# A two-block transformer kernel: first loads on two queues, one load for x and its weights, new durations in the list scheduler

## The chip, the core and the metric

The kernel runs on 1 core of one Trainium2 chip. A core has five engines with instruction streams of their own: PE (TensorE, matmuls), DVE (VectorE), ACT (ScalarE), POOL (GpSimd) and SP (SyncE, which here only issues loads and stores). The metric is the device time of one execution in microseconds (us), the median of the runs; lower is better.

## The reference

256 rows of 1,024 features pass through two transformer blocks in f32. What the start of the program computes is the first normalisation and the first product:

```
def rmsnorm(x, w):
    xf = x.astype(jnp.float32)
    y = xf * lax.rsqrt(jnp.mean(xf * xf, axis=-1, keepdims=True) + EPS)
    return (y * w.astype(jnp.float32)).astype(x.dtype)

def first_block(x, attn_norm_w, w_in, ...):
        h = rmsnorm(x, attn_norm_w[l])
        proj = h @ w_in[l]
        (q_a, k_a, v_a, q_b, k_b, v_b, g_b, g_c, x_c) = jnp.split(proj, split_points, axis=-1)
        y_sb = from_heads(stick_breaking_attention(to_heads(q_a), to_heads(k_a), to_heads(v_a)))
        qh = rmsnorm(to_heads(q_b), q_norm_w[l])
        kh = rmsnorm(to_heads(k_b), k_norm_w[l])
        y_ch = from_heads(chunked_relpos_attention(qh, kh, to_heads(v_b), rel_bias[l]))
        y_cv = short_conv_mixer(g_b, g_c, x_c, conv_w[l])
        y = group_rmsnorm(jnp.concatenate([y_sb, y_ch, y_cv], axis=-1), out_norm_w[l])
        x = x + y @ w_out[l]
        x = x + swiglu(rmsnorm(x, ffn_norm_w[l]), w_gate[l], w_up[l], w_down[l])
    return x
```

The second block (a gated spatial mixer, a dilated attention, a convolved feed-forward part) follows in the same way. About 124 MB of weights and tables are read once.

## The kernel before, in words

**Tiles.** The 256 rows are two tiles of 128 (t = 0 and 1). Every product is done as three f32r products: the operands are split into a rounded high part and a low part (the remainder), and high by high, low by high and high by low are added up in PSUM. x comes already transposed (`xT`, features on the partitions), in four pieces of 256 KB: `xT00` and `xT01` are the two halves of the features for t = 0, `xT10` and `xT11` those for t = 1 (first digit t, second digit the half). `first_half` loads a piece, multiplies it by the norm's weights (`vec`, a table of all such weights), makes the high part on ACT and the low part on DVE. The row scale of the norm comes from X (x, not transposed) and is put on later, when the sums leave PSUM.

**Weights.** They stand in DRAM in the order of use, cut into units of 512 KB (256 features by 512 columns). `load_stream` (L499) issues them on SP into a ring of 4 buffers (`raw`); `hi_stream` makes the high part on ACT (`whi`), `lo_stream` the low part on DVE (`wlo`), each in a ring of 8. A unit costs each row tile 6 matmuls of 128x512 (4 with `whi`, 2 with `wlo`). Units 0 and 1 (`FINE = 2`) are loaded and split in two halves of 256 KB, a and b below. The table `START` (L33) says ahead of which unit the other first loads are issued. Nine bf16 matmuls on zeros (`warm`, `WARM = 9`) run ahead of everything on PE.

**Order.** The program is written by a list scheduler (`Kit.run`, L385): streams of operations are Python generators, every operation has an engine and an estimated duration, and the one that could start first by these estimates is written next. So the estimates decide the order of every engine's instructions, and on the chip each engine works in that order, waiting on semaphores. `evac` (L341) also uses the estimates: what has to leave PSUM goes to ACT or to DVE, whichever is free first. `get` gives out buffers of a ring in the same way, by the estimated time at which they come free.

**Queue.** All loads and stores are issued on SP. Its stream is in order too: an issue whose buffer isn't free yet holds up all issues behind it.

Of the kernel before, what the change touches and what calls it, by code (L numbers as in the profile page):

```python
# [13 lines left out]
ALU = mybir.AluOpType  # L14
# [18 lines left out]
START = {0: ("xT00",), "half": ("xT00b",), 1: ("xT10",), 3: ("xT01",), 4: ("xT11",), 5: ("X0",), 7: ("X1",),  # L33
         8: ("W", "cst"), 9: ("rel",), 16: ("cw",)}
# [134 lines left out]
class Op:  # L169
    __slots__ = ("eng", "cost", "ins", "outs", "fn", "table")  # L170

    def __init__(self, eng, cost, ins, outs, fn, table=None):
        self.eng, self.cost, self.fn, self.table = eng, cost, fn, table
        self.ins = [x.cell for x in ins if isinstance(x, T)]
        self.outs = [x.cell for x in outs if isinstance(x, T)]
# [13 lines left out]
class Kit:  # L189


    def __init__(self, nc, pool, psum):
        self.nc, self.pool, self.psum = nc, pool, psum
        self.clk = {e: 0.0 for e in ("pe", "act", "dve", "pool", "dma")}
# [60 lines left out]
    def mm(self, *items, also=()):  # L255
        cost, ins, outs = 0.0, list(also), []
        for out, a, b, start, stop in items:
# [4 lines left out]
            elif dt == BF16:  # L262
                cost += 0.42e-3 * max(n, 64)
            elif raw(out).shape[0] == 64:
                cost += 0.133
            else:
                cost += 4 * 0.417e-3 * max(n, 128)
# [9 lines left out]
    def tr(self, ident, *items):  # L277
# [4 lines left out]
        return Op("pe", 0.106 * len(items), [a for _, a in items], [o for o, _ in items], fn)  # L282
# [66 lines left out]
    def dma(self, out, in_, eng="dma", nbytes=None):  # L349
# [20 lines left out]
    def emit(self, op, start):  # L370
# [6 lines left out]
        if op.eng == "dma":  # L377
            end += 2.0
# [35 lines left out]
def build(ctx, tc, a):  # L414
# [48 lines left out]
    qk8 = fixed("qk8", [P, 2])  # L463
    stats = fixed("stats", [P, 256])
# [34 lines left out]
    def load_stream():  # L499
        def first(*names):  # L500
            for n in names:
                if n == "W":
# [5 lines left out]

        for p in range(NU):
# [153 lines left out]
    def run_units(t, seq, pt, tag, fin, src=None):  # L663
# [3 lines left out]
        for i, (name, c, u) in enumerate(seq):  # L667
# [6 lines left out]
            else:  # L674
                if i == 0 and (t, tag) == (0, "n1"):
                    yield from k.until("px0")
                    xs = [(px[0][0][:, j], px[0][1][:, j]) for j in (0, 1)]
# [688 lines left out]
    px = {}  # L1366

    def first_half(t, h, pt, ss):
# [3 lines left out]
        yield from k.until(f"go_xT{t}{h}")  # L1372
        xw = yield from k.get("xw", [P, 4, P])
        cuts = [(0, 2), (2, 4)] if (t, h) == (0, 0) else [(0, 4)]
        parts = [xw.part((slice(None), slice(i, j))) for i, j in cuts]
        if len(cuts) == 2:
            yield k.dma(vec, a["vec"])
        for (i, j), part in zip(cuts, parts):
            if i:
                yield from k.until("go_xT00b")  # L1380
            yield k.dma(part, a["xT"][:, t, 4 * h + i:4 * h + j])
            k.done(f"xT{t}{h}" + ("b" if i else ""))
        for (i, j), part in zip(cuts, parts):
            w = V_ATTN + 4 * h
            hi, lo = pt[h][1][:, i:j], pt[h][2][:, i:j]
            if len(cuts) == 2:
                hi, lo = [T(v.ap, Cell()) for v in (hi, lo)]
                px[i // 2] = (hi, lo)
            yield k.tt(part, part, vec[:, w + i:w + j].bc(2, [P, j - i, P]), ALU.mult)
            yield k.act(hi, part)  # L1390
            yield k.tt(lo, part, hi.f32(), ALU.subtract)
            if len(cuts) == 2:
                k.done(f"px{i // 2}")
        k.free(xw, *parts)
        if len(cuts) == 2:
# [319 lines left out]
```

## Time and profile before

| | |
|---|---|
| median of 3 runs | 707.07 us (706.31 to 707.54) |
| profiled execution, its own time | 707.77 us |
| its span, first to last instruction | 706.0 us |
| PE busy | 688.6 us (98% of the span) |
| DVE busy | 488.1 us (69%) |
| ACT busy | 395.5 us (56%) |
| POOL busy | 59.6 us (8%) |
| read from HBM | 123.94 MB |

The profile is of one execution. Between its span and its own time lie 1.77 us outside the first and the last instruction, and its own time is 0.70 us above the median of the runs. Busy is the share of time in which an engine has an instruction under way; a matmul that runs at half clock counts as busy for twice as long.

### The profile page before, as it was taken

What the parts mean: (1) busy time and instruction counts of PE and PEld (TensorE: products, weight loads), DVE (VectorE), ACT (ScalarE), POOL (GpSimd) and SP (SyncE); (2) the same over time, 40 slices, a digit from 0 to 9 for tenths busy, and PEclk for the clock granted to TensorE, in tenths of its full rate; (3) what the DMA queues carried; (4) which work ended last, traced back from release to release, by engine and by line L of the source; (5) the groups of instructions that cost most, each with busy time, mean ns of one, the idle gap of its engine ahead of it and who ended that gap; (6) DMA issues with size and microseconds to landing.
All of it is one profiled execution on the core that took longest, in us unless ns stands there. A gap on an engine that the chain in (4) does not pass through costs nothing.

```text
span 706.0 us, 9657 instructions
## 1 busy us (share of the span) xinstructions
PE 688.6 (98%) x3535; PEld 573.3 (81%) x3535; DVE 488.1 (69%) x743; ACT 395.5 (56%) x614; POOL 59.6 (8%) x105
## 2 busy tenths in 40 slices
PE   7999999999999999999999999999999999999995
PEld 3878777888888888888887888888888888888884
DVE  5666777687666666686567556457777878777773
ACT  4667674565545544574457647444546756555542
POOL 0461433010000000011000000000011000000001
PEclk8999999999999999999999999999999999999998
DMA  7883435555555555565454355665454555555531
GB/s 217 323 273 120 146 121 186 180 208 176 174 208 185 182 180 182 196 228 167 139 187 154 94 179 174 213 206 179 162 179 167 172 178 189 179 191 197 188 110 60
DMA packets 38392, 126.17 MB, mean 179 GB/s; under 512 B 4668, under 2 KB 6856, under 8 KB 38344
## 3 DMA queue, kind: packets, MB, share of 16 engines
q1 hardware_dynamic: 38344, 125.54, 53.0%
q8 instruction: 28, 0.46, 0.3%
q14 instruction: 20, 0.16, 0.1%
HBM read 123.94 MB, written 1.06 MB: 177 GB/s over the span
## 4 chain that ended last, share of the span: by engine, by line
PE 89%; DMA 4%; DVE 2%; ACT 2%; issue 1%; POOL 1%; SPq 0%; POOLq 0%; ACTq 0%; DVEq 0%
PE acc L273 50%; PE work L273 35%; PE work L280 3%; DMA raw<-in_weights 2%; DVE wlo L301 1%; ACT whi L293 1%; DMA xw<-in_xT 1%; DMA uvB<-uvA 1%; POOL stats L301 1%; ACT xw L293 0%; SPq L355 0%; DVE X L301 0%; DVE xw L301 0%; POOL uvB L301 0%; ACT s L293 0%
## 5 line engine op out<-in xcount | busy, mean ns | idle before, releaser
L301 DVE TENSOR_TENSOR wlo<-raw,whi 128x1024 fp32r<-128x1024 f32 (+1 forms) x230 | 275.8, 1208 | 86.9 <-ACT whi L293 69.0
L293 ACT ACTIVATE whi<-raw 128x1024 fp32r<-128x1024 f32 (+1 forms) x230 | 235.1, 1042 | 102.9 <-PE acc L273 74.8
L273 PE MATMUL acc<-whi,xb 128*128 128x512 f32 (+1 forms) x768 | 201.1, 392 | 4.0 <-ACT whi L293 3.8
L273 PEld LDWEIGHTS acc<-whi,xb 128*128 128x128 f32 x768 | 141.4, 189 | 36.0 <-ACT whi L293 6.9
L273 PE MATMUL work<-xb,whi 128*128 128x512 f32 x576 | 143.4, 391 | 0.0
L273 PEld LDWEIGHTS work<-xb,whi 128*128 128x128 f32 x576 | 105.9, 188 | 20.6
L273 PE MATMUL acc<-wlo,xb 128*128 128x512 f32 (+1 forms) x384 | 116.0, 398 | 3.1 <-DVE wlo L301 3.1
L273 PEld LDWEIGHTS acc<-wlo,xb 128*128 128x128 f32 x384 | 69.3, 190 | 18.3 <-DVE wlo L301 4.9
L273 PEld LDWEIGHTS work<-xb,wlo 128*128 128x128 f32 x576 | 78.5, 190 | 5.6
L273 PE MATMUL work<-xb,wlo 128*128 128x256 f32 x576 | 80.4, 282 | 0.0
L301 POOL TENSOR_SCALAR stats<-stats 128x1 f32<-128x1 f32 (+3 forms) x36 | 15.3, 424 | 592.5 <-ACT xw L293 555.2
L273 PE MATMUL acc<-whi,qkb 128*128 128x512 f32 x224 | 59.7, 390 | 0.0
L273 PEld LDWEIGHTS acc<-whi,qkb 128*128 128x128 f32 x224 | 41.3, 188 | 8.1
L293 ACT ACTIVATE qka<-work 128x256 f32<-128x256 f32 (+1 forms) x56 | 19.5, 380 | 43.3 <-PE work L273 38.7
L273 PE MATMUL acc<-wlo,qkb 128*128 128x512 f32 x112 | 34.6, 393 | 0.0
L301 DVE TENSOR_TENSOR qka<-work,qka 128x256 f32<-128x256 f32 (+1 forms) x56 | 22.1, 419 | 17.3 <-ACT qka L293 17.2
L273 PE MATMUL acc<-whi,y 128*128 128x512 f32 x96 | 25.9, 391 | 0.0
L301 POOL TENSOR_TENSOR stats<-stats,half 128x1 f32<-128x1 f32 (+3 forms) x26 | 25.0, 960 | 2.0
L293 ACT ACTIVATE xb<-xw 128x512 fp32r<-128x512 f32 (+1 forms) x21 | 12.8, 610 | 21.4 <-DVE xw L301 21.3
L293 ACT ACTIVATE xw<-X 128x512 bf16<-128x512 f32 x20 | 12.5, 626 | 20.9 <-DVE X L301 20.9
L273 PEld LDWEIGHTS acc<-wlo,qkb 128*128 128x128 f32 x112 | 20.5, 188 | 3.9
L301 DVE TENSOR_TENSOR qka<-qka,s 128x512 f32<-128x512 f32 x27 | 18.7, 693 | 6.2 <-ACT qka L293 5.6
(204 smaller groups left out, 642.9 us busy)
## 6 DMA issues: line engine op xcount, KB each, us to landing
raw<-in_weights SPq DMA_DIRECT2D x222, 512.0 KB, 4.1
raw<-in_weights SPq DMA_DIRECT2D x8, 256.0 KB, 2.6
X<-in_x SPq DMA_DIRECT2D x4, 256.0 KB, 6.3
s<-relext SPq DMA_DIRECT2D x4, 256.0 KB, 5.4
out<-y SPq DMA_DIRECT2D x4, 256.0 KB, 2.1
xw<-in_xT SPq DMA_DIRECT2D x3, 256.0 KB, 6.8
cB<-in_final_norm_g SPq DMA_DIRECT2D x1, 512.0 KB, 5.4
uvB<-uvA SPq DMA_DIRECT2D x4, 112.0 KB, 3.8
```

The source lines that it names most:

```text
L273: self.nc.tensor.matmul(raw(out), raw(a), raw(b), start=start, stop=stop, skip_group_check=True)
L280: self.nc.tensor.transpose(raw(out), raw(a), raw(ident))
L293: self.nc.scalar.activation(raw(out), raw(in_), func, scale=raw(scale), **kw)
L301: getattr(e, meth)(*[raw(x) for x in a], **{k: raw(v) for k, v in kw.items()})
```

## The change

1. The first piece of x and the first eight norm weights become one array, `xT00`, of 520 floats per partition, loaded by one transfer; the load of `vec` moves from the first place to the one ahead of unit 5. The load of unit 0's first half is issued by ACT, all others by SP.
2. ACT's activation table is loaded by a small activation on `half` ahead of the wait for x. The four blocks of 128 columns of the first piece are scaled and rounded by ACT, one activation each (`activation` with a scale per partition), and DVE makes each low part from the unscaled x in one operation (`scalar_tensor_tensor`). The matmuls of t = 0 wait for blocks, not for pieces. The other pieces use a copy of the weights made on POOL (`wn1`).
3. `xT10` and `xT11` land in the buffers `yb0` and `yb1`, no longer in the ring `xw`.
4. The scheduler's estimates change: a load costs its issue (0.45), then a wire that all loads share (1.4 and the bytes at 330 GB/s); the clocks start at 0.7; small f32 matmuls, transposes, POOL and the first nine matmuls get other durations.

```diff
-START = {0: ("xT00",), "half": ("xT00b",), 1: ("xT10",), 3: ("xT01",), 4: ("xT11",), 5: ("X0",), 7: ("X1",),
-         8: ("W", "cst"), 9: ("rel",), 16: ("cw",)}
+START = {1: ("xT10",), 3: ("xT01",), 4: ("xT11",), 5: ("vec",), 6: ("X0",), 7: ("X1",), 8: ("W", "cst"), 9: ("rel",), 16: ("cw",)}
+
+D_ISSUE, D_LAT, D_BYTE, T0 = 0.45, 1.4, 1 / 330e3, 0.7
...
-            return 0.12 + 2.2e-3 * n
+            return 0.28 + 2.2e-3 * n
...
-            self.nc.sync.dma_start(raw(out), raw(in_))
-
-        return Op(eng, max(nbytes / 360e3, 0.1), [in_], [out], fn)
+            (self.nc.scalar if eng == "act" else self.nc.sync).dma_start(raw(out), raw(in_))
+
+        return Op(eng, D_ISSUE, [in_], [out], fn, nbytes=nbytes)
...
-        if op.eng == "dma":
-            end += 2.0
+        if op.nbytes:
+            self.wire = end = max(self.wire, end + D_LAT) + op.nbytes * D_BYTE
...
+        yield from k.until("x00")
         for p in range(NU):
             yield from first(*START.get(p, ()))
             r = yield from k.get("raw", [P, 2, width[p]])
             rawt[p] = (r, halves(r, p))
             for i, d in enumerate(rawt[p][1]):
-                yield k.dma(d, src_of[p] if p >= FINE else src_of[p][:, i:i + 1])
-                if p == 0 and i == 0:
-                    yield from first(*START["half"])
+                yield k.dma(d, src_of[p] if p >= FINE else src_of[p][:, i:i + 1], "dma" if p or i else "act")
...
-        cuts = [(0, 2), (2, 4)] if (t, h) == (0, 0) else [(0, 4)]
...
+        if (t, h) == (0, 0):
+
+            xs = yield from k.get("s", [P, 4 * P + 8])
+            yield k.dma(xs, a["xT00"])
+            k.done("x00")
+            w8 = xs[:, 4 * P:4 * P + 8]
+
+            yield from k.until("half")
+            yield k.act(qk8[:, 0:1], half[:, 0:1])
+            px = PX[t]
+            for i in range(4):
+                px[i] = [T(pt[h][n].ap[:, i], Cell()) for n in (1, 2)]
+                src, sc = xs[:, P * i:P * i + P], w8[:, i:i + 1]
+                yield k.act(px[i][0], src, AF.Copy, sc)
+                yield k.stt(px[i][1], src, sc, px[i][0].f32(), ALU.mult, ALU.subtract)
+                k.done(f"px{t}{i}")
+            yield k.copy(wn1, w8, "pool")
...
+            xw = yield from k.get(f"yb{h}" if t else "xw", [P, 4, P])
+            yield k.dma(xw, a["xT"][:, t, 4 * h:4 * h + 4])
+            k.done(f"xT{t}{h}")
+            yield from k.until("w8")
+            yield k.tt(xw, xw, wn1[:, 4 * h:4 * h + 4].bc(2, [P, 4, P]), ALU.mult)
```

What the change does to the order of the instructions stands in the built programs. First SP's stream, from its start, before. Names are tiles (`raw_0` is the first buffer of the ring `raw`, the numbers behind it count uses), `xw`, `s` and `yb0` are the buffers that x lands in, sizes are partitions by elements:

```order
L355 DMA vec_74<-in_vec 128x134
L355 DMA xw_0_20_99<-in_xT 128x256
L355 DMA raw_0_24_104<-in_weights 128x512
L355 DMA xw_0_20_99<-in_xT 128x256
L355 DMA raw_0_24_104<-in_weights 128x512
L355 DMA xw_1_29_117<-in_xT 128x512
L355 DMA raw_1_30_124<-in_weights 128x512 x2
L355 DMA raw_2_32_132<-in_weights 128x1024
L355 DMA xw_0_34_142<-in_xT 128x512
L355 DMA raw_0_35_150<-in_weights 128x1024
L355 DMA xw_1_37_156<-in_xT 128x512
L355 DMA raw_1_41_171<-in_weights 128x1024
```

SP's stream from its start, of the change:

```order
L357 DMA s_1_20_100<-in_xT00 128x520
L357 DMA raw_0_24_104<-in_weights 128x512
L357 DMA yb0_0_26_108<-in_xT 128x512
L357 DMA raw_1_27_113<-in_weights 128x512 x2
L357 DMA raw_2_31_121<-in_weights 128x1024
L357 DMA xw_0_32_124<-in_xT 128x512
L357 DMA raw_3_33_128<-in_weights 128x1024
L357 DMA yb1_0_34_133<-in_xT 128x512
L357 DMA raw_0_37_154<-in_weights 128x1024
L357 DMA vec_74<-in_vec 128x134
L357 DMA raw_1_40_174<-in_weights 128x1024
```

Three issues have gone from the front (`vec`, a half of x, a half of unit 0, which is ACT's now). Unit 3 took the buffer of unit 0 (`raw_0`) and takes the unused fourth one now (`raw_3`); no piece of x lands any more in a buffer that another piece had, where `xT01` and `xT11` did.

ACT's stream from its start, before:

```order
L293 ACT_TABLE_LOAD
L293 ACTIVATE xb0_67<-xw_0_20_99 128x256
L293 ACTIVATE whi_0_25_105<-raw_0_24_104 128x512
L293 ACTIVATE xb0_67<-xw_0_20_99 128x256
L293 ACTIVATE whi_0_25_105<-raw_0_24_104 128x512
L293 ACTIVATE xb0_67<-xw_1_29_117 128x512
L293 ACTIVATE whi_1_33_140<-raw_1_30_124 128x512 x2
```

ACT's stream from its start, of the change:

```order
L357 DMA raw_0_24_104<-in_weights 128x512
L295 ACT_TABLE_LOAD
L295 ACTIVATE qk8_78<-half_75 128x1
L295 ACTIVATE xb0_67<-s_1_20_100 128x128 x4
L295 ACTIVATE whi_0_25_105<-raw_0_24_104 128x512 x2
L295 ACTIVATE whi_1_36_147<-raw_1_27_113 128x512
L295 ACTIVATE xb0_67<-yb0_0_26_108 128x512
L295 ACTIVATE whi_1_36_147<-raw_1_27_113 128x512
```

All four blocks of x stand ahead of the first `whi` now, where one half of them did; the table load was ACT's first instruction already.

Third, DVE in the attention part of the first block, t = 1 (`pt` is the transposed softmax, copied out of PSUM; `y1` its output), before:

```order
L301 TENSOR_TENSOR wlo_6_156_787<-raw_2_125_593,whi_6_155_785 128x1024
L301 TENSOR_TENSOR uvA0_0_8_87<-uvA0_0_8_87,uvB0_0_9_88 128x256
L301 ISA s_0_154_772,stats_79<-work_0_151_763,cA_0_73_332 128x256
L301 ISA stats_79 128x1
L301 RECIPROCAL stats_79<-stats_79 128x2
L301 TENSOR_TENSOR wlo_7_161_817<-raw_0_139_670,whi_7_159_814 128x1024
```

The same place in DVE's stream, of the change:

```order
L303 TENSOR_TENSOR wlo_6_148_749<-raw_2_122_579,whi_6_147_742 128x1024
L303 TENSOR_TENSOR uvA0_0_8_88<-uvA0_0_8_88,uvB0_0_9_89 128x256
L303 COPY pt_2_149_756<-work_0_141_695 128x512
L303 RECIPROCAL stats_80<-stats_80 128x2
L303 COPY pt_3_154_779<-work_2_142_696 128x512
L303 RECIPROCAL stats_80<-stats_80 128x2
L303 TENSOR_TENSOR wlo_7_153_773<-raw_3_131_635,whi_7_152_771 128x1024
```

Copies of `pt` that ACT made stand on DVE now: in this part of the program DVE has 5 of them where it had 2, and two more products of 256 columns leave PSUM by DVE. PE's matmuls are the same ones. Of the 1,986 rows of its stream, the order differs from the 28th to about the 216th (the first block up to its output product), from the 1,029th to the 1,155th (the second block's attention) and in one row further on; the rest is the same, the end included.

## Rows read from the trace of the kernel before

**Rows 1.** The page: PE's busy time, its share of the span, its instructions.

```profile
PE 688.6 (98%) x3535; PEld 573.3 (81%) x3535; DVE 488.1 (69%) x743; ACT 395.5 (56%) x614; POOL 59.6 (8%) x105
```

**Rows 2.** PE's waits, whole run: us in total, times, the longest.

```profile
PE acc L273 <- ACT whi L293: 3.8, 2, 2.4
PE acc L273 <- DVE wlo L301: 3.1, 3, 1.4
...
PE work L280 <- DVE qkb L301: 1.0, 1, 1.0
```

**Rows 3.** Timeline from the start: start, us, engine, line, operation, tiles [idle before <-releaser].

```profile
0.71 1.28 ACT L293 ACT_TABLE_LOAD   x1 [0.71 <-PEq L1705]
0.72 0.39 SPq L355 DMA_DIRECT2D vec<-in_vec  x1
...
1.17 4.02 PE L273 MATMUL work<-pt 128*128 128x512 bf16 x9 [1.17 <-DVE pt L301]
...
2.58 0.43 SPq L355 DMA_DIRECT2D raw<-in_weights  x1
...
5.31 0.73 PE L273 MATMUL acc<-whi,xb 128*128 128x512 f32 x2
...
7.79 0.63 ACT L293 ACTIVATE whi<-raw 128x512 fp32r<-128x512 f32 x1 [1.70 <-DMA raw<-in_weights]
...
8.47 1.12 PE L273 MATMUL acc<-whi,xb 128*128 128x512 f32 x2 [2.42 <-ACT whi L293]
...
10.69 0.68 DVE L301 TENSOR_TENSOR wlo<-raw,whi 128x512 fp32r<-128x512 f32 x1
...
11.41 0.33 SPq L355 DMA_DIRECT2D raw<-in_weights  x1
...
11.43 0.80 PE L273 MATMUL acc<-wlo,xb 128*128 128x512 f32 x1 [1.42 <-DVE wlo L301]
...
15.53 1.53 PE L273 MATMUL acc<-whi,xb 128*128 128x512 f32 x6
```

**Rows 4.** Longest pieces of the chain after 60 us: start, us, what.

```profile
437.65 44.94 PE acc L273 x198
```

**Rows 5.** Stretches: us, busy us (instructions) of each engine, granted clock, DMA.

```profile
core 0: us, PE busy (x) PEld busy (x) DVE busy (x) ACT busy (x) POOL busy (x), PEclk, DMA share, GB/s
0.00:1.70 1.70, 0.53 (x2) 0.26 (x3) 0.27 (x1) 0.99 (x1) 0.79 (x7) 1.00 0.00 0
1.70:5.20 3.50, 3.49 (x9) 0.90 (x7) 0.85 (x2) 1.17 (x3) 0.00 (x0) 1.00 0.76 213
5.20:8.60 3.40, 0.86 (x3) 0.43 (x4) 1.36 (x3) 1.10 (x3) 0.00 (x0) 1.00 0.88 189
8.60:12.00 3.40, 1.98 (x4) 0.88 (x4) 1.82 (x3) 1.19 (x3) 0.00 (x0) 0.50 0.75 292
12.00:15.50 3.50, 3.50 (x9) 2.80 (x9) 3.50 (x6) 2.17 (x3) 0.00 (x0) 0.51 0.77 239
...
20.00:27.00 7.00, 6.94 (x31) 5.30 (x30) 3.67 (x3) 5.78 (x13) 3.26 (x9) 1.00 1.04 393
...
80.00:120.00 40.00, 36.93 (x202) 30.53 (x201) 29.60 (x53) 24.21 (x44) 12.01 (x19) 1.00 0.46 154
```

**Rows 6.** Groups by shape, ACT and DVE: xcount | busy us, mean ns.

```profile
L293 ACT ACTIVATE whi<-raw 128x512 fp32r<-128x512 f32 x8 | 4.9, 624 | 4.2 <-PE acc L273 2.5 <-DMA raw<-in_weights 1.7
...
L293 ACT ACTIVATE vb<-vb,vec 128x128 f32<-128x128 f32 x8 | 3.0, 396 | 0.8 <-DVE vb L301 0.8
...
L293 ACT ACTIVATE yb<-work 128x128 fp32r<-128x128 f32 x4 | 1.1, 277 | 1.8 <-PE work L273 1.7
...
L301 DVE SCALAR_TENSOR_TENSOR vb<-xw,vec,vb 128x128 f32<-128x128 f32 x16 | 5.6, 350 | 0.4
...
L301 DVE COPY pt<-work 128x512 f32<-128x512 f32 x5 | 3.4, 685 | 0.8 <-PE work L280 0.8
```

**Rows 7.** DMA issues from 3.5 to 6 us: KB each, median us to landing.

```profile
raw<-in_weights SPq DMA_DIRECT2D x2, 256.0 KB, 7.2
```

More of the change, by code (lines that the diff above doesn't have):

```diff
@@ L169, with __init__ @@
 class Op:
[L170 to L173 removed]
+    __slots__ = ("eng", "cost", "ins", "outs", "fn", "table", "nbytes")
+    def __init__(self, eng, cost, ins, outs, fn, table=None, nbytes=0):
+        self.eng, self.cost, self.fn, self.table, self.nbytes = eng, cost, fn, table, nbytes
         self.ins = [x.cell for x in ins if isinstance(x, T)]
@@ L252, in spawn, with mm @@
         self.streams.append([prio, gen, None])
-    def mm(self, *items, also=()):
-        cost, ins, outs = 0.0, list(also), []
+    def mm(self, *items, also=(), more=0.0):
+        cost, ins, outs = more, list(also), []
         for out, a, b, start, stop in items:
@@ L263, in mm @@
                 cost += 0.42e-3 * max(n, 64)
-            elif raw(out).shape[0] == 64:
-                cost += 0.133
+            elif raw(out).shape[0] == 64 or raw(a).shape[0] == 64:
+                cost += 0.108 if n <= 128 else 2 * 0.422e-3 * n
             else:
-                cost += 4 * 0.417e-3 * max(n, 128)
+                cost += 0.224 if n <= 128 else 4 * 0.422e-3 * n
             ins += [a, b]
@@ L501, in first @@
             for n in names:
-                if n == "W":
+                if n == "vec":
+                    yield k.dma(vec, a["vec"])
+                    k.done("vec")
+                elif n == "W":
                     yield k.dma(W, a["cst"][:, C_W + 2:C_W + P + 2])
@@ L674, in run_units @@
             else:
-                if i == 0 and (t, tag) == (0, "n1"):
-                    yield from k.until("px0")
-                    xs = [(px[0][0][:, j], px[0][1][:, j]) for j in (0, 1)]
+                if u < 2 and (t, tag) == (0, "n1"):
+                    yield from k.until(f"px{t}{2 * u}", f"px{t}{2 * u + 1}")
+                    xs = [PX[t][2 * u], PX[t][2 * u + 1]]
                 else:
@@ L1371, in first_half @@
         pt[h] = (x, x.part((slice(None), 0)), x.part((slice(None), 1)))
-        yield from k.until(f"go_xT{t}{h}")
-        xw = yield from k.get("xw", [P, 4, P])
-        cuts = [(0, 2), (2, 4)] if (t, h) == (0, 0) else [(0, 4)]
[L1375 to L1393, printed above, removed]
@@ L1394, in first_half @@
-        k.free(xw, *parts)
-        if len(cuts) == 2:
+        if (t, h) == (0, 0):
[13 more added lines that the diff above has]
+            yield k.copy(wn1, w8, "pool")
+            k.done("w8")
@@ L1396, in first_half @@
             for n in (1, 2):
-                pt[h][n].cell.w = max(px[0][n - 1].cell.w, px[1][n - 1].cell.w)
+                pt[h][n].cell.w = max(px[i][n - 1].cell.w for i in range(4))
                 pt[h][n].cell.eng = "act" if n == 1 else "dve"
+            k.free(xs)
+        else:
+            yield from k.until(f"go_xT{t}{h}")
+            xw = yield from k.get(f"yb{h}" if t else "xw", [P, 4, P])
[3 more added lines that the diff above has]
+            yield k.tt(xw, xw, wn1[:, 4 * h:4 * h + 4].bc(2, [P, 4, P]), ALU.mult)
+            yield k.act(pt[h][1], xw)
+            yield k.tt(pt[h][2], xw, pt[h][1].f32(), ALU.subtract)
+            k.free(xw)
@@ L1559, in setup @@
         yield k.memset(half, -0.5, "pool")
+        k.done("half")
         yield from k.until("x0")
@@ L1629, in warm @@
         for i in range(WARM):
-            yield k.mm((b, z[:, 0:P], z, True, True))
+            yield k.mm((b, z[:, 0:P], z, True, True), more=0.21)
         k.free(b)
@@ L1694 @@
         "xT": v["x"].reshape(2, P, 8, P).transpose(3, 0, 2, 1),
+        "xT00": np.concatenate([v["x"].reshape(2, P, 8, P).transpose(3, 0, 2, 1)[:, 0, 0:4].reshape(P, 4 * P),
+                                vec[:, 0:8]], axis=1),
         "vec": vec,
```

8 lines of the change are left out of this document (5 added, 3 removed).

## The prediction

> **What bounds the kernel now.** I read the page first: PE is busy in 98% of the span [rows 1], so a change can gain where PE waits, where it runs at half clock, or by fewer matmuls. The matmuls are the same. The list of PE's waits [rows 2] shows three kinds: for the rounded weights (`whi`, 3.8 us in 2 waits), for the remainders (`wlo`, 3.1 us in 3) and one of 1.0 us for `qkb`. The timeline [rows 3] puts the longest of the first two kinds into the first 12 us: 2.42 us ahead of 8.47 and 1.42 us ahead of 11.43. That leaves 1.4 + 1.7 + 1.0 = 4.1 us for all that comes later.
>
> The start costs more than these waits. The first real matmul starts at 5.31, and the six that start at 15.53 come after 2+2+1+1+6+2 = 14 of them (the timeline's rows between, of which [rows 3] shows the ends of the waits). Far on in the run, 198 matmuls of the same size take 44.94 us, 0.227 us each [rows 4]. So 15.53 - 5.31 = 10.22 us did 14 x 0.227 = 3.18 us of work: **7.04 us are lost**, 3.84 in the two waits and 3.2 in matmuls that took twice as long. The stretches [rows 5] show why: the granted clock is 1.00 until 8.6 us, 0.50 from 8.6 to 12.0 and 0.51 to 15.5, that is 1.2 GHz in place of 2.4; PE had been busy for 0.86 of 3.40 us before it fell, and for a whole stretch before it came back.
>
> Why is the data late? The second half of unit 0 is issued as the fifth load, at 2.58 us, and ACT waits for it until 7.79 [rows 3]. The DMA engines are busy for 0.76 to 0.88 of the time from 1.7 us on but move 189 to 292 GB/s, where they move 393 at 20 to 27 us [rows 5]; the halves of unit 1 land 7.2 us after their issue [rows 7]. And unit 3, which took unit 0's buffer, is issued at 11.41, when the second `wlo` of unit 0, begun at 10.69, is through [rows 3]; SP had been standing at this row with all later loads behind it.
>
> **The change part by part, against the 7.04 us.**
>
> *First matmul.* The piece of x (266 KB) and the first half of unit 0 (262 KB) go out together at about 0.72 us, from two queues. The engines begin to move data at 1.7 us [rows 5]. 528 KB take 1.34 us at 393 GB/s and 2.48 us at 213: x is there between 3.1 and 4.2, I take 3.7. Then ACT has four blocks of 128 columns, for which the trace has 277 ns without and 396 ns with an operand per partition [rows 6]: 1.1 to 1.6 us, I take 1.3, nearer to the second since these have a scale. Then `whi`, 0.62 [rows 6]: 5.65 us, against 5.31. **+0.3 us** (from -0.1, since the nine matmuls on zeros end at 1.17 + 4.02 = 5.19 [rows 3], to +1.1).
>
> The Trainium skill, "DMA: Bandwidth & Descriptors", section "Issuing engines are not separate DMA queues", says that loads started from several engines run on the same 16 DMA engines and interleave, and that only the time to start them is saved. By that rule the sum is the one above; if the second queue had engines of its own, x would land after its own 266 KB, at 2.4 to 2.9 us, and the first matmul would wait for the matmuls on zeros alone, at 5.2. No run so far has loads on two queues.
>
> *Issues and the table.* The issue on ACT takes some 0.4 us as SP's do, ahead of a table load of 1.28 [rows 3]; both end at about 2.4, before x is there, as the dummy activation does. The table load was over early before, too: this part is worth nothing, and would cost 0.4 us if x landed before 2.4. `vec` (69 KB, 0.2 us at 393 GB/s) goes from the first place on SP to the one ahead of unit 5; its next reader, on POOL, stands behind the row sums of X, which are loaded later still. POOL's copy of the weights runs while `xT10`, its first user's other operand, is on its way; without that cover it would cost its own few tenths. Nothing is taken for these.
>
> *The second half of unit 0* is second in SP's queue. 790 KB are through at 3.7 (393 GB/s) to 5.4 us (213 GB/s). Its `whi` follows the first on ACT, at 6.3. DVE's four remainders of x take 0.35 us each [rows 6], beside ACT's blocks, and end before it. The wait of 2.42 us is gone, and t = 0 has its six matmuls of unit 0 done at about 7.3.
>
> *Unit 1.* Next come `xT10` and the halves of unit 1, up to 1,314 and 1,577 KB. At the rates of the trace (1.7 to 5.2: 745 KB; to 8.6: 643 more; then 292 GB/s [rows 5]) they land at 8.2 and 9.25; at 393 GB/s at 5.1 and 5.7. I take 7.0 and 8.0, between the two, since the slow stretch has less to explain it when issues don't stand still. With 0.62 for `whi`, PE gets its matmuls at 7.6 and 8.6, and unit 2 (2,101 KB, 7.1 to 11.0, then 1.06 us of `whi`) just about as it is through with these and with t = 1 on unit 0. PE's order here is that of before. **2.0 us of waits are left** (0.3 to 3.9), for 3.84. Units 3 and 4 and both other pieces of x have free buffers or nearly so; from there on the loads should keep ahead: a unit lasts 12 x 0.227 = 2.7 us on PE and 524 KB take 2.2 us even at 239 GB/s.
>
> *Clock.* Before, 0.86 us of matmul stood in the 3.4 us ahead of the fall; now it would be some 2. Whether that holds the clock no row says: the 1.98 us in the next stretch, already at half clock, did not bring it back. Lost is nothing, or half of a stretch of 3.4 us, 1.7, or both stretches as before, 3.3. I take half of 1.7: **0.9 us**.
>
> Sum of the start: 0.3 + 2.0 + 0.9 = 3.2 us lost for 7.04: **3.8 us gained.**
>
> *The new estimates* change the order up to the attention of the first block, and in the second block's, where PE has no wait to win. Three more copies of `pt` at 0.685 us [rows 6] and two products of 256 columns move from ACT to DVE: 2.1 us for the copies alone, 3.0 with the others at half a copy and more each, on an engine that is busy for 29.6 of 40 us from 80 to 120 us [rows 5]. PE waits for `wlo` there, but the 4.1 us of later waits could as well shrink under better estimates. I take **0** (from -2.0 to +3.0).
>
> The profiled execution had 707.77 us of its own, 706.0 of span; 707.77 - 3.8 = 704.0. The median of the runs lies 0.70 below that execution: **703.3 us.**
>
> **The rivals.**
>
> *Loads keep up* (700.7 us). If the DMA engines move 393 GB/s from the start, unit 1 is there at 5.7, only 0.3 us of waits and the 0.3 of the start are left, and the clock stays: 6.4 us gained. For it: nothing holds SP any more. Against it: share 0.88 at 189 GB/s [rows 5] are busy engines with slow transfers, not missing ones.
>
> *The clock falls anyway* (705.6 us). With the clock at 0.50 from 8.6 to 15.4 as before, 0.3 + 2.0 + 3.3 = 5.6 us are lost, 1.4 to 1.5 gained. For it: waits of 2 us stay in the same stretch. The Trainium skill, "TensorE: Matmul & The Clock Gate", section "HAM oscillation", describes just this, bursts of matmuls between waits for loads, each begun at half clock. The trace agrees, at 0.50 after the waits.
>
> *Given back* (707.0 us). The attention part hangs on DVE and ACT; if its length is set by their chain and not by when PE comes, PE waits there for what it gained. For it: the later waits are all for these two. Against it: they are 4.1 us in all, so PE mostly has other matmuls there while a chain runs.
>
> *Slower* (710.0 us): the same part has DVE as its bound, and the 3.0 us moved to DVE lengthen it; the front's gain is waited away there. It needs DVE's 10.4 idle us in 40 [rows 5] to be waits for others throughout, and decides as soon as less than 3.0 us of the front's gain gets through.
>
> **How the numbers follow.** Forecast 0.54 (701.5 to 705.2 its own range), loads keep up 0.20, clock falls 0.10, given back 0.09, slower 0.07. A measurement tells about 0.2% here, 1.4 us. Faster: 0.54 + 0.20 + half of 0.10 = 0.79; the same: 0.05 + 0.09 = 0.14; slower: 0.07. The range for 8 in 10 leaves out the slower case, half of "given back" and the best third of "loads keep up", 0.07 + 0.045 + 0.07: 700.2 to 706.9.
>
> **What would show it.** First real matmul at 5.2 to 6.4 us; PE's second wait no longer for a load of unit 0 but for unit 1, shorter than 2.4 us; SP's issue of unit 3 before 6 us instead of 11.41; the 15th real matmul 3 to 5 us earlier than 15.53, and the end of the run by as much. Granted clock above 0.50 at 12.0 to 15.5. If the start gains and the end doesn't, new waits on DVE between 40 and 120 us are to be seen. Wrong it would be if loads on two queues slowed each other, so that x lands after 4.2 us, or if PE's new order waits for units that land later than the estimates' 330 GB/s.

## The result and the profile after

The change takes **699.55 us** (698.75 to 699.87, 4 runs) where the kernel before takes 706.69 (706.21 to 707.54, 4 runs) beside it: a ratio of 0.9896 [0.9879, 0.9913]. It is faster by 7.1 us; 3.8 were forecast, and 699.55 lies below the range. A second measurement, beside the last experiments, gave 700.29 us, just inside the range, and 0.9917 [0.9899, 0.9935]: 6.4 us by the medians, 5.9 by the ratio. Gains below are differences of medians; the ratios, with their 95% intervals, can differ from them by some 0.5 us. The profiled execution has 699.36 us of its own and a span of 697.6. That of before was 1.1 us above its median, so the two traces differ by 8.4 us, not by 7.1.

The page of the change, the line of busy times [rows 1] and two of the DMA queues (packets, MB, share); q10 is ACT's load, which is new:

```profile
PE 684.8 (98%) x3535; PEld 572.0 (82%) x3535; DVE 489.0 (70%) x748; ACT 393.3 (56%) x612; POOL 61.2 (9%) x106
...
q1 hardware_dynamic: 38056, 125.29, 53.0%
...
q10 hardware_dynamic: 144, 0.26, 0.1%
```

PE's waits in the change, whole run [rows 2]:

```profile
PE acc L275 <- ACT whi L295: 2.7, 3, 1.3
PE work L275 <- DVE pt L303: 1.2, 1, 1.2
PE work L275 <- DVE y L303: 1.0, 1, 1.0
```

The wait for `pt` is the first one, at 1.17 us, for the zeros of the nine warm matmuls. Waits for `wlo` and for `qkb` are gone. The timeline of the change from the start [rows 3]:

```profile
0.71 0.40 ACTq L357 DMA_DIRECT2D raw<-in_weights  x1
...
0.72 0.39 SPq L357 DMA_DIRECT2D s<-in_xT  x1
...
4.24 1.27 ACT L295 ACTIVATE xb<-s 128x128 fp32r<-128x128 f32 x4 [1.59 <-DMA s<-in_xT]
...
4.41 0.57 SPq L357 DMA_DIRECT2D raw<-in_weights  x1
...
5.42 1.13 ACT L295 ACTIVATE whi<-raw 128x512 fp32r<-128x512 f32 x2
...
6.08 1.24 PE L275 MATMUL acc<-whi,xb 128*128 128x512 f32 x4 [1.15 <-ACT whi L295]
...
7.16 0.75 PE L275 MATMUL acc<-wlo,xb 128*128 128x512 f32 x2
...
8.52 0.63 ACT L295 ACTIVATE whi<-raw 128x512 fp32r<-128x512 f32 x1 [1.96 <-DMA raw<-in_weights]
...
9.20 0.74 PE L275 MATMUL acc<-whi,xb 128*128 128x512 f32 x2 [1.28 <-ACT whi L295]
...
10.24 1.19 PE L275 MATMUL acc<-whi,xb 128*128 128x512 f32 x4 [0.31 <-ACT whi L295]
...
11.73 1.07 PE L275 MATMUL acc<-whi,xb 128*128 128x512 f32 x4
```

The row at 11.73 begins with the 15th real matmul (real are all behind the nine on zeros). Before, it came at 15.53 [rows 3]: the start has gained 3.80 us. Unit 3's load is issued at 4.41 where it was 11.41. The stretches of the change [rows 5]:

```profile
1.70:5.20 3.50, 3.23 (x9) 0.93 (x7) 0.53 (x2) 1.90 (x6) 0.19 (x1) 1.00 0.96 274
5.20:8.60 3.40, 1.83 (x6) 0.97 (x6) 2.68 (x6) 1.44 (x5) 0.00 (x0) 1.00 0.96 297
8.60:12.00 3.40, 2.50 (x10) 1.76 (x11) 2.76 (x5) 2.79 (x5) 0.00 (x0) 1.00 1.04 417
12.00:15.50 3.50, 3.50 (x17) 2.92 (x16) 3.50 (x5) 2.78 (x4) 0.00 (x0) 1.00 1.02 313
...
80.00:120.00 40.00, 38.75 (x205) 31.40 (x204) 31.26 (x55) 23.38 (x42) 17.65 (x19) 1.00 0.46 156
```

The granted clock is 1.00 to 15.5, where it was 0.50 from 8.6 to 15.5. The record of the clock begins at 4.54 us in this trace and at 5.19 in that of before, and the view gives 1.00 for what lies ahead of it. The matmuls there say otherwise: in before the nine on zeros take 4.02 us [rows 3], 0.45 each, and seven of the same shape in e8 below take 1.69, 0.24 each, so the nine run at half clock. From 80 to 120 us DVE is busy for 1.7 us more (31.26 for 29.60), and so is PE (38.75 for 36.93): what moved to DVE doesn't hold PE up.

Where the 8.4 us between the traces come from is read off the starts of numbered matmuls, which are the same products in both. The 15th real one is 3.80 us earlier, the 47th (18.99 for 23.19) 4.20, the 1,527th (303.77 for 311.43, in the second block) 7.66, the last (689.55 for 698.04) 8.49. **Half of the gain is made after the loads have caught up.**

### The profile page after: what moved, and what is told of

Same layout as the page of the kernel before. It is cut to its first block, busy times and chain, and to the rows that moved or that the text cites. A ratio compares the mean times of both kernels' runs of the same rounds, so it can differ in the third digit from the quotient of the medians.

```text
span 697.6 us, 9658 instructions
## 1 busy us (share of the span) xinstructions
PE 684.8 (98%) x3535; PEld 572.0 (82%) x3535; DVE 489.0 (70%) x748; ACT 393.3 (56%) x612; POOL 61.2 (9%) x106
## 4 chain that ended last, share of the span: by engine, by line
PE 84%; DVE 1%; ACT 0%; POOL 0%; issue 0%; POOLq 0%; ACTq 0%; DVEq 0%
PE acc L275 47%; PE work L275 34%; PE work L282 2%; DVE X L303 0%; POOL stats L303 0%; ACT xw L295 0%; PE acc L282 0%; DVE wlo L303 0%; ACT whi L295 0%; ACT y L295 0%; DVE pt L303 0%; DVE xw L303 0%; DVE uvA L303 0%; POOLq L1724 0%; DVE s L303 0%
## 5 line engine op out<-in xcount | busy, mean ns | idle before, releaser
L295 ACT ACTIVATE vb<-work 128x256 f32<-128x256 f32 x18 | 6.7, 380 | 25.4 <-PE work L275 25.4
```

The lines of the kernel that those rows point to most:

```text
L295: self.nc.scalar.activation(raw(out), raw(in_), func, scale=raw(scale), **kw)
```

## The experiments

All times are medians; each kernel was run beside the kernel before on one chip (706.87 us for e1 to e4, 707.01 for e5 to e8, 706.78 for e9 to e12, 706.70 for e13 to e16). "Idle" is PE's idle time after 20 us in the profiled execution, gaps over 0.08 us added up; "15th" is the start of the 15th real matmul.

| run | us (runs) | ratio to before [95%] | 15th | idle |
|---|---|---|---|---|
| before | 706.69 (4) | 1 | 15.53 | 4.6 |
| the change | 699.55 (4) | 0.9896 [0.9879, 0.9913] | 11.73 | 1.2 |
| e16, the change again | 700.29 (5) | 0.9917 [0.9899, 0.9935] | 12.13 | 1.4 |
| e1, parts 1 to 3 alone | 705.99 (12) | 0.9990 [0.9979, 1.0001] | 11.56 | 6.2 |
| e2, part 4 alone | 702.67 (6) | 0.9936 [0.9922, 0.9951] | 14.77 | 1.2 |
| e3, before, fourth buffer first | 706.44 (12) | 0.9995 [0.9982, 1.0008] | 14.94 | 2.5 |
| e4, the change, one queue | 702.96 (6) | 0.9938 [0.9922, 0.9953] | 14.24 | 1.6 |
| e8, e4 with fillers | 700.85 (6) | 0.9912 [0.9893, 0.9932] | 12.60 | 1.4 |
| e5, the change, old PE durations | 701.89 (6) | 0.9926 [0.9906, 0.9946] | 11.55 | 2.6 |
| e6, the change, old POOL duration | 701.58 (6) | 0.9918 [0.9895, 0.9940] | 11.98 | 2.1 |
| e7, the change, old load estimate | 704.49 (8) | 0.9957 [0.9941, 0.9972] | 12.90 | 3.3 |
| e13, e1 with new PE durations | 704.11 (11) | 0.9965 [0.9953, 0.9978] | 11.54 | 4.7 |
| e14, e1 with new POOL duration | 703.96 (8) | 0.9961 [0.9944, 0.9978] | 12.55 | 3.2 |
| e15, e1 with new load estimate | 702.90 (5) | 0.9950 [0.9933, 0.9966] | 12.56 | 2.5 |
| e9, the change, PE number nudged | 703.77 (12) | 0.9960 [0.9946, 0.9973] | 11.77 | 3.3 |
| e10, the change, DVE number nudged | 700.08 (6) | 0.9910 [0.9893, 0.9927] | 11.82 | 1.5 |
| e11, before, PE number nudged | 710.65 (5) | 1.0056 [1.0044, 1.0068] | 14.96 | 6.0 |
| e12, e1, PE number nudged | 706.96 (12) | 1.0010 [0.9999, 1.0020] | 11.17 | 7.5 |

### The two halves of the change (e1, e2, e3)

e1 has the loads, the table and the buffers of the change, but the scheduler's old estimates:

```diff
-D_ISSUE, D_LAT, D_BYTE, T0 = 0.45, 1.4, 1 / 330e3, 0.7
+D_ISSUE, D_LAT, D_BYTE, T0 = 0.45, 1.4, 1 / 330e3, 0.0
...
-                cost += 0.224 if n <= 128 else 4 * 0.422e-3 * n
+                cost += 4 * 0.417e-3 * max(n, 128)
...
-            return 0.28 + 2.2e-3 * n
+            return 0.12 + 2.2e-3 * n
...
-        return Op(eng, D_ISSUE, [in_], [out], fn, nbytes=nbytes)
+        return Op(eng, max(nbytes / 360e3, 0.1) if eng == "dma" else 0.1, [in_], [out], fn, nbytes=nbytes)
...
-            self.wire = end = max(self.wire, end + D_LAT) + op.nbytes * D_BYTE
+            end += 2.0
```

> The changed first loads (parts 1 to 3 of the change) with the old durations in the scheduler. Theory A: the change has two gains, the start (15th real matmul 3.8 us earlier) and, apart from it, an order of the later instructions that the new durations made (about 4 us of later waits gone). Then this kernel gains the first alone: 702 to 703.5 us, 15th real matmul near 11.7 us, later waits of TensorE of 3 us or more as before. Theory B: the later waits went because the start is earlier, whatever the durations: 699 to 700.5 us, later waits near 1 us.

e2 is the other half, the kernel before with the estimates of the change (the same lines the other way round):

> The new durations in the scheduler (part 4) with the old first loads. Theory A (two separate gains): 702 to 703.5 us, the 15th real matmul near 15.5 us as before, and TensorE's waits after 20 us down from 4.1 to about 1 us. Theory B (all comes from the start): 706 to 707.5 us, later waits as before.

e3 leaves the kernel before as it is, but for the choice among buffers that are equally free, which prefers one that nobody had:

```diff
-        s = min(free, key=lambda s: s[2])
+        s = min(free, key=lambda s: (s[2], s[3] is not None))
```

> The kernel before with one edit: on equal estimates the ring gives out the buffer that was never used, so that unit 3 goes into the fourth buffer and its issue does not wait for unit 0's remainders. Order otherwise the same. Theory A: unit 3 is issued when its queue slot is free, some 4 us earlier than 11.41, but TensorE's first two waits are for unit 0, so it is worth 0 to 0.7 us. Theory B: this issue, which held up all later loads, is the main cause of the late start: 2 to 4 us gained (702.7 to 704.7).

Theory A held in e2 and in e3. In e1 it is right on the start and on the later waits, and wrong on the time, for which theory B was wrong, too. e1 gains the whole start: its 15th real matmul is at 11.56, its clock stays at 1.00. Of the 4.0 us only 0.9 reach the end of the run, by an interval that just takes in 1. e2 starts almost as before (14.77) and is 4.2 us faster. The two alone add up to 5.1 of the 7.1 us: the new order is worth more on the new loads. The rival "given back" was what the loads do by themselves. Of e3, unit 3 is issued at 6.96 instead of 11.41, and that brings nothing that can be told (0.4 us).

Where e1 loses it again the timeline shows (`qkb` holds q and k of the chunked attention, whose row statistics are worked out on POOL and put on by DVE); PE's rows with a wait between 14 and 130 us, all but two short ones:

```profile
30.97 0.65 PE L282 MATMUL work<-W,qkb 128*128 128x128 f32 x4 [1.53 <-DVE qkb L303]
37.43 0.66 PE L282 MATMUL work<-W,qkb 128*128 128x128 f32 x4 [0.33 <-DVE qkb L303]
45.41 0.66 PE L282 MATMUL work<-W,qkb 128*128 128x128 f32 x4 [0.91 <-DVE qkb L303]
...
95.93 0.73 PE L275 MATMUL acc<-wlo,xb 128*128 128x512 f32 x2 [1.42 <-DVE wlo L303]
...
115.00 1.20 PE L275 MATMUL acc<-whi,xb 128*128 128x512 f32 x4 [0.91 <-ACT whi L295]
```

What stands ahead of the first of them, in e1's timeline of all engines from 26.8 us on:

```profile
26.82 1.33 POOL L303 COPY s<-s 8x127 f32<-8x127 f32 x1
...
28.23 0.20 POOL L303 TENSOR_SCALAR stats<-stats 128x8 f32<-128x8 f32 x1
...
28.52 1.68 POOL L303 TENSOR_TENSOR stats<-stats,half 128x8 f32<-128x8 f32 x1
...
28.83 0.61 PE L275 MATMUL acc<-wlo,xb 128*128 128x512 f32 x2
...
30.23 0.69 DVE L303 TENSOR_TENSOR qkb<-qkb,stats 128x512 f32<-128x512 f32 x1 [2.22 <-POOL stats L303]
```

The row statistics stand on POOL behind a copy of 8x127 that took 1.33 us; the old estimate for it is 0.12 + 2.2e-3 x 127 = 0.40, the new one 0.56. The order has PE turn to the transposes of `qkb` before POOL and DVE are through. That the estimate of POOL is why is likely, but not shown by these rows: the same copy takes 0.28 us in the change, where it stands behind other work of POOL, which is less than either estimate. The same place in the change, PE's timeline:

```profile
28.96 2.01 PE L275 MATMUL acc<-whi,xb 128*128 128x512 f32 x8
30.81 1.08 PE L275 MATMUL acc<-wlo,xb 128*128 128x512 f32 x4
31.73 0.60 PE L282 MATMUL work<-W,qkb 128*128 128x128 f32 x4
```

No bracket, no wait: PE has more matmuls in front of the transposes here, and it gets to them later than e1 did, with nothing lost.

### The second queue and the clock (e4, e8)

e4 is the change with ACT's load on SP's queue too; the order of all else is that of the change.

```diff
-            (self.nc.scalar if eng == "act" else self.nc.sync).dma_start(raw(out), raw(in_))
+            self.nc.sync.dma_start(raw(out), raw(in_))
```

> The changed kernel with the first half of unit 0 issued by SyncE, behind the piece of x, instead of by ScalarE; order otherwise the same. Theory A (both queues share the DMA engines): x lands earlier by some tenths and the half of unit 0 later by as much, time within 0.5 us of the change's 699.55. Theory B (the second queue is worth a piece of the start): 0.7 to 1.5 us slower than the change, since all later issues on SyncE move back by 0.4 us and the half of unit 0 by more.

It gains 3.9 us on the kernel before where the change gains 6.4 to 7.1: one queue costs 2.5 to 3.2 us, more than either theory had. The clock was in neither. The timeline of e4:

```profile
3.54 1.28 ACT L295 ACTIVATE xb<-s 128x128 fp32r<-128x128 f32 x4 [1.33 <-DMA s<-in_xT]
...
5.39 1.20 PE L275 MATMUL acc<-whi,xb 128*128 128x512 f32 x2 [0.20 <-ACT whi L295]
...
7.12 0.74 PE L275 MATMUL acc<-whi,xb 128*128 128x512 f32 x2 [0.53 <-ACT whi L295]
...
10.47 0.80 PE L275 MATMUL acc<-whi,xb 128*128 128x512 f32 x1 [2.13 <-ACT whi L295]
```

and its stretches:

```profile
5.20:8.60 3.40, 2.42 (x6) 1.17 (x6) 1.39 (x3) 0.77 (x2) 0.00 (x0) 1.00 0.86 248
8.60:12.00 3.40, 1.53 (x3) 0.99 (x4) 2.24 (x4) 1.91 (x4) 0.00 (x0) 0.68 1.04 414
12.00:15.50 3.50, 3.50 (x9) 2.65 (x9) 3.42 (x6) 2.42 (x4) 0.00 (x0) 0.50 0.97 326
```

On one queue x lands 0.70 us earlier (3.54 for 4.24), since the weights go behind it and not beside it; unit 1 is at PE 1.27 us later (10.47 for 9.20), and the clock falls, from 9.84 to 16.67 us by the record of the trace. The 1.27 are of two single traces: in e16, on two queues, unit 1 is at PE at 9.60, and in e8, on one, at 10.07, which is 0.47 apart, as much as its load is issued later (2.58 us for 2.10). e8 takes data and clock apart: seven bf16 matmuls on zeros, which add nothing to the sums, stand in e4's wait ahead of unit 1.

```diff
+                if raw(b).dtype == F32R:
+                    self.real = getattr(self, "real", 0) + 1
+                    for i in range(7 if self.real == 7 else 0):
+                        self.nc.tensor.matmul(raw(out), raw(self.z)[:, 0:P], raw(self.z), start=False, stop=False, skip_group_check=True)
```

> The change with all loads on SP's queue (702.96 us), and seven bf16 matmuls on zeros that add nothing to the sums put ahead of unit 1's first matmul, where PE waits 2.13 us. They take some 1.6 us at full clock, so they fit the wait. Theory A (of the 3.4 us that one queue costs, 1.3 are unit 1's later data and 2.1 the granted clock, 0.5 from 9.84 to 16.67): the clock stays at 1.00 and the time comes to 700.5 to 701.3. Theory B (the clock follows the late data whatever PE does, or the 3.4 us are all late data): 702.5 to 703.5. If the fillers run at half clock they delay unit 1 by up to 1 us: above 703.

The timeline of e8:

```profile
7.24 1.69 PE L278 MATMUL acc<-pt 128*128 128x512 bf16 x7
10.07 0.73 PE L279 MATMUL acc<-whi,xb 128*128 128x512 f32 x2 [1.15 <-ACT whi L299]
```

and its stretches:

```profile
5.20:8.60 3.40, 3.34 (x13) 2.03 (x13) 1.30 (x2) 0.53 (x2) 0.00 (x0) 1.00 0.88 261
8.60:12.00 3.40, 1.94 (x8) 1.05 (x7) 2.59 (x5) 2.31 (x4) 0.00 (x0) 1.00 1.04 416
```

The clock stays at 1.00, and e8 gains 6.2 us on before: some 2.3 of what one queue costs are the clock, and 0.2 to 1.0 the later data. Theory A of e8 held. The 2.3 are rough: the intervals of e4 and e8 just overlap, and unit 1 was there 0.40 us earlier in e8's trace than in e4's. That it is the clock the other executions say, too: its mean over the run is 0.992 to 0.996 in all six of e4, and 0.997 or 0.998 in four of e8, whose other two (0.994 and 0.995) are its slowest. e8 does not beat the change.

### Which of the new durations (e5 to e7, e13 to e15)

e5, e6 and e7 put one group of durations back in the change; the diffs are the lines of e1, in this order: PE's, POOL's, the loads'.

> The change with one group of its new durations put back: those of small f32 matmuls, transposes and the first nine matmuls (PE). The rest of the estimates and all loads are the change's. Theory P (corrected durations are worth what they are right about): the durations of PE decide when its next operand is needed, so putting them back costs most of the 5 us that the new order gave: 703 to 705. Theory L (the loads' estimates and the start clock do it): 699 to 700.5. Theory S (any new number only writes another order, and orders scatter): anything from 699 to 706, with PE's waits after 12 us longer by as much as the time, and no link to which number was put back.

> The change with POOL's old duration (0.12 for its fixed part, in place of 0.28). Theory P and theory L alike: POOL does 59.6 us of work in all, so this is nearly no loss: 699 to 700.5. A theory Q, that POOL's steps in the row statistics are estimated too early and what follows them is written too early: 702 to 704, with waits of PE behind POOL's results. Theory S: anything from 699 to 706.

> The change with the old estimate of a load (bytes at 360 GB/s on its queue and 2.0 more, no shared wire) and clocks that start at 0. Durations of PE and POOL are the change's. Theory L: back to about the loads-only version, 704 to 706.5, with waits after 12 us of 4 to 6 us. Theory P: 699 to 701. Theory S: anything from 699 to 706. At the start nothing changes for t = 0; PE reads unit 1's second remainder ahead of t = 1's matmuls there, so up to 0.5 us more wait before 12 us by all of them.

e13, e14 and e15 are the other way round: e1 with one group of the new durations.

> The loads-only version (705.99 us) with the new PE durations alone; POOL and loads as of before. Theory G (each group takes away its own waits; those for qkb at 30 to 46 us, 2.8 us in the loads-only version, hang on POOL's row statistics): these waits stay, 704 to 706. Theory T (any one group does, since each single one could be put back without the waits at 30 to 46 us coming again): they are gone, 700 to 703.5. Theory S (order by chance): waits after 12 us anywhere from 1 to 6 us.

> The loads-only version with POOL's new duration alone. Theory G: the waits for qkb at 30 to 46 us are gone, 2.8 us less, 702 to 704. Theory T: 700 to 703.5. Theory S: as above, and the waits for qkb stay or go without a pattern over these three runs.

> The loads-only version with the new estimate of a load and clocks from 0.7 alone. Theory G: the waits for qkb stay, 704 to 706; the wait for wlo at 45 to 60 us may go, since a unit is expected later. Theory T: 700 to 703.5. Theory S: as above.

> The change itself, once more, beside the three above, so that they and the earlier ones can be set against it on one chip. By every theory 699 to 700.3. If it comes to more than 700.8, the four runs of the first measurement were on the fast side, and what one queue and the single groups cost shrinks by as much.

Set against before on their own chips, e1 gains 0.9, e13 2.6, e14 2.7 and e15 3.8 us: PE's durations bring 1.7 us more, POOL's 1.9, the loads' 2.9, together 6.5, where all three bring 5.5 (by e16) to 6.3 (by the first measurement). Putting one back costs 1.3 to 2.0, 1.0 to 1.7 and 3.9 to 4.6. The loads' estimate is the largest both ways, but **no one group does it**, and theories P and L, that one would, both fall. Theory Q falls with e6 (701.58, with 0.3 us of waits for `qkb`), G with e15, T with e13 and e14. These numbers hold some of the start as well: in e7, e14 and e15 the 15th real matmul comes 0.8 to 1.2 us later than in the change, and in the traces of e7 and e14 the clock falls there for 3.4 us (from 9.07 and from 11.04). Two things go with a group in the traces:

- The waits for `qkb` between 30 and 46 us. They stay with PE's new durations alone, as in e13's timeline:

```profile
30.72 0.66 PE L282 MATMUL work<-W,qkb 128*128 128x128 f32 x4 [1.22 <-DVE qkb L303]
```


They are 2.5 us in e13, 2.8 in e1 and 3.2 in e12, and at most 0.24 us in e14 and e15 and in e5 to e7, which all have POOL's new duration or the loads' new estimate. The rows above make a reason for POOL's likely; why the loads' does it too is not shown by a row. e3 has none of these waits with old durations throughout, so the group isn't the only way to be rid of them.

- The second block's attention. From the 1,527th real matmul to the last, the ten traces with PE's new durations take 385.7 to 386.1 us (385.78 in the change), the eight with the old ones 386.4 to 386.8 (386.61 before). That is 0.8 us by PE's durations alone, with no wait in PE's timeline there. Some 0.6 of it are matmuls of 64 rows (`work<-kTb,qTb`), which mostly start in pairs, 7 ns apart. In before eight of them stand in one row at 384.58, which takes 1.83 us, and the last four of the eight start one by one, some 0.3 us apart; in the change they stand in two rows of four with other matmuls between, at 376.85 and 380.27, of 0.60 and 0.70 us, all in pairs. All eight traces with the old durations have these four single starts, and none of the ten with the new ones. What keeps the four apart isn't shown.

### A trifle in one number (e9 to e12)

The scheduler decides by comparing estimated starts, so any other number writes another order. e9, e11 and e12 have half a per cent more on a large matmul, in the change, in before and in e1; e10 has 1 ns more on a DVE operation, in the change:

```diff
-                cost += 0.0135 + 0.4167e-3 * n
+                cost += 0.0135 + 0.4187e-3 * n
...
-        return 0.065 + 1.05e-3 * n + 0.055 * isinstance(scalar, T)
+        return 0.066 + 1.05e-3 * n + 0.055 * isinstance(scalar, T)
```

> The change with one number of the estimates moved by a trifle: 0.4187 in place of 0.4167 ns a column for f32r matmuls, half a per cent, which is neither righter nor wronger than before by what a row shows. Theory S (any other number writes another order, and orders scatter): the order differs, and the time comes out somewhere from 700 to 704, with PE's waits after 12 us longer by about as much. Theory R (the new durations are righter, and an order by right durations is good, whichever it is): 699 to 700.5, waits after 12 us of 1 to 1.5 us.

> The change with DVE's estimate moved by 1 ns an operation (0.066 for 0.065). Theory S: 700 to 704, other than the change and than the first nudge by up to some us. Theory R: 699 to 700.5.

> The kernel before with the same trifle on f32r matmuls. Its first instructions stay as they are, so what changes is the order of the attention parts. Theory S: 703 to 709, to either side of the kernel before, by the waits after 12 us (4.6 us in it). Theory R: within 1 us of the kernel before, since the old durations are as wrong as they were.

> The loads-only version (705.99 us; new loads, old estimates) with the same trifle on f32r matmuls. Theory S: the 4.1 us that its start gains may come through now: anything from 700.5 to 707, by the waits after 12 us (6.2 us in the loads-only version). Theory R: 705 to 707, the start's gain is given back again.

e10 is the change again (6.7 us gained). e9 gains only 3.0, and **e11 is 3.9 us slower than before**: a number that is no righter and no wronger moves the time by up to 4 us. e9's loss is one place, its timeline there:

```profile
108.10 1.49 DVE L303 TENSOR_TENSOR uvA<-uvA,uvB 128x256 f32<-128x256 f32 x1 [2.05 <-POOL uvB L303]
109.51 1.21 DVE L303 TENSOR_TENSOR xb<-xw,xb 128x512 fp32r<-128x512 f32 x1
...
110.64 0.47 DVE L303 TENSOR_SCALAR uvA<-acc,stats 128x256 f32<-128x256 f32 x1
...
111.15 0.47 ACT L295 ACTIVATE va<-acc,stats 128x256 f32<-128x256 f32 x1 [3.49 <-DVE uvA L303]
...
111.68 2.61 PE L275 MATMUL work<-va,s 128*128 128x64 f32 x16 [2.76 <-ACT va L295]
```

and the stretches around it:

```profile
108.00:112.80 4.80, 2.04 (x14) 1.51 (x14) 4.70 (x6) 1.10 (x2) 2.69 (x4) 1.00 0.07 29
112.90:116.20 3.30, 3.30 (x12) 2.91 (x12) 2.56 (x6) 0.69 (x2) 0.69 (x3) 0.50 0.65 234
116.30:120.00 3.70, 3.70 (x21) 3.02 (x20) 2.17 (x4) 1.67 (x3) 2.80 (x4) 1.00 0.07 27
```

One wait of 2.76 us, and behind it 3.4 us at half clock: it costs twice, as the start of before did. (`va` and `uvA` are products of the first block that leave PSUM by ACT and DVE.) PE waits for `va`, ACT's `va` for DVE's `uvA`, and DVE, busy for 4.70 of 4.80 us, had two other operations ahead of it, of which the first had waited for POOL.

This execution, 702.61 us, is among the three fastest of e9's twelve, which have a mean clock of 0.995 over the run; the other nine have 0.990 to 0.993 and take 703.10 to 706.86 us. In e11's trace, too, the clock falls once more than in before, at 100.4 us, behind a wait of 1.37 us for `wlo`.

So theory S (orders scatter) holds, with a reach of 0 to 4 us; e11 lies even beyond the bound that it set. Theory R, that any order by right durations is good, falls with e9, and with e11, which it had within 1 us of before. A weaker form of it is left: on the new loads the orders by all the new durations gain 3.0, 6.4 to 7.1 and 6.7 us, those by the old ones 0.9 and -0.2; on the old loads 4.2 against 0 and -3.9. In every such pair the new durations win, by 2.1 to 8.1 us.

## Why the prediction was wrong

**What bounds, and the 7.04 us.** Right. The start now loses 11.73 - 5.31 - 3.18 = 3.24 us against the old first matmul's time, where 3.2 were forecast; the gain there is the forecast 3.8 (3.40 in the trace of e16). That the sum fits so well is luck: its terms are 0.77, 1.59 and 0.88 us where 0.3, 2.0 and 0.9 were taken, and the last is not what it was taken for.

**First matmul.** Mis-sized by 0.4: 6.08, not 5.65. x landed at about 4.2, at the bound of the range and of what was to show the prediction wrong, not at 3.7; ACT's four blocks took 1.27 as reckoned. The rule of the Trainium skill that loads from several engines share the same DMA engines ("DMA: Bandwidth & Descriptors", "Issuing engines are not separate DMA queues") agrees: beside the weights x lands at 4.24, alone in front (e4) at 3.54, and not at the 2.4 to 2.9 of queues with engines of their own. Whether only issue time is saved, as that section of the Trainium skill also says, the runs leave open. From 1.7 to 8.6 us the change moves 3.5 x 274 + 3.4 x 297 = 1,969 KB, e4 on one queue 3.5 x 250 + 3.4 x 248 = 1,718 KB, but by the same stretches e8, on one queue too, moves 3.5 x 273 + 3.4 x 261 = 1,843 KB, about as much as e16 on two (3.5 x 258 + 3.4 x 283 = 1,865); unit 1 comes forward by 0.47 (e16 against e8) to 1.27 us (the change against e4), of which the issue that SP is spared makes up to 0.48.

**Second half of unit 0, unit 1.** Right in kind: the wait of 2.42 is gone, the second wait is for unit 1, and 1.28 + 0.31 = 1.59 us are left where 2.0 were taken. The size is luck: with PE through at 7.3 and the halves at 7.6 and 8.6, the prediction's own times make some 0.3 + 0.5 us of waits, not 2.0. In the trace PE is through at 7.9 and gets unit 1 at 9.20, since its first half landed at 8.5 and not at 7.0.

**Clock.** Taken at 0.9 us, measured 0 in the trace, where the granted clock is 1.00 as far as the record goes. Over the whole run it is 0.997 or 0.998 in seven of the change's nine executions and 0.996 in two of e16's, one of which is its slowest (702.26 us). That the waits need not bring it down was left open by the rows. With e4's wait of 2.13 us it fell, with e8's work in that wait it did not. The prediction's "1.00 until 8.6 us" is a misreading: until 5.19 there is no record, and the matmuls on zeros ran at half clock. It does no harm to the sum. In e6 and e9 the record begins at 9.38 and 10.48 us only, and their first six real matmuls start 0.42 to 0.60 us apart, yet the 15th comes at 11.98 and 11.77, since unit 1 isn't there before.

The 0.9 us that were taken for the clock stand elsewhere, beside the waits. From the start of one row of the timeline to the next, less the idle time in brackets, the 14 matmuls take 1.08 (four), 0.76 (two), 0.73 (two) and 1.49 us (six), 4.06 in place of 3.18. The two rows of two, which end in a wait, have 0.3 us each too much: a wait costs that much more here than its bracket says. In the trace the first matmul behind each of the three waits takes 0.34 us to the next one's start, and not 0.227.

The section "HAM oscillation" of the Trainium skill's "TensorE: Matmul & The Clock Gate" tells of bursts of matmuls between waits for loads, each begun at half clock. That fits before and e4, at 0.50 behind waits of 2.42 and 2.13 us, and not the change, at 1.00 behind waits of 1.15 and 1.28.

**The new estimates, the step that failed.** "I take **0** (from -2.0 to +3.0)": alone they are worth 4.2 us (e2), on the new loads 5.5 to 6.3 (the change against e1), both outside its bounds. Nothing in the rows gave the 0; it was a choice in the middle of what was feared and hoped. Two assumptions behind it were wrong. The first was that the 4.1 us of later waits are all that an order can give or take: 0.8 us more lie in the second block, where the prediction saw "no wait to win". With the idle time after 20 us, which falls from 4.6 to 1.2, that is the 4.2 of e2. The second was that the start's gain keeps its size whatever the order is: under the old estimates only 0.9 of 4.0 us come through (e1), so the new order also had 3 us to save from being lost: on the new loads the idle time falls from 6.2 to 1.2, which with the 0.8 is 5.8. Put at 3.3 us, the difference of 7.1 and 3.8, the step would have given the measured time, just beyond its own upper bound; by the second measurement it is 2.6, just within.

**What was feared of DVE** did not come. It has 1.7 us more from 80 to 120 us, the waits for its `pt` and `y` after 20 us are 1.1 us in all, and the time from 47th to 1,527th matmul is 3.5 us shorter (284.78 for 288.24).

**The rivals.** "Loads keep up" (700.7) is nearest to the measured time, but by another way: its 6.4 us of gain at the start are 3.8. "Given back" (707.0) is what the loads alone do, and "the clock falls anyway" (705.6) is what e4 shows on one queue. "Slower" has its mechanism, a wait for a DVE that has too much before it, in e9, not in the change.

**What stays open.** How much of the 5.5 to 6.3 us is owed to righter durations and how much to the luck of this order: a nudge takes 4 us away (e9) or nothing (e10). The signs are the same in all pairs, of which there are few, and the size isn't settled.

## What to carry to other kernels

Where a list scheduler writes the program, its estimates are part of the kernel: an edit's gain at one place comes through only if the order behind it lets it, so time the edit under both sets of estimates, and take a difference of less than the scatter of trifles (here up to 4 us of 707) for no verdict on the edit. A PE wait in the trace is to be priced with the clock behind it: 2.76 us of wait brought 3.4 us at half clock. And filling a wait with matmuls on zeros kept the clock where the data couldn't come earlier (some 2 us in e8).

## What was not expected of the hardware

In all eighteen traces the DMA engines are slow for a short while some 5 us after the start, at 130 to 211 GB/s from 5.1 to 6.8 us, whatever is issued; the change's stretches, and e4's:

```profile
5.10:6.80 1.70, 0.72 (x3) 0.49 (x4) 1.53 (x5) 1.45 (x4) 0.00 (x0) 1.00 0.88 181
6.80:8.50 1.70, 1.11 (x5) 0.48 (x3) 1.25 (x2) 0.00 (x0) 0.00 (x0) 1.00 1.02 396
8.50:10.20 1.70, 0.74 (x2) 0.30 (x2) 1.02 (x2) 1.67 (x3) 0.00 (x0) 1.00 1.04 417
```

```profile
5.10:6.80 1.70, 1.29 (x3) 0.50 (x2) 0.79 (x2) 0.60 (x2) 0.00 (x0) 1.00 0.67 130
```

181 and 130 GB/s stand between stretches of 299 and 396 in the change and of 237 and 345 in e4. By the bytes moved until then it is `xT10` and the first half of unit 1 that travel. What slows them isn't shown, and no run tried it.
